# Which weight sums of a feed-forward are made by accumulating transfers, and where the second product stands

## The chip, the cores and the metric

The kernel runs on one core of one Trainium2 chip. The metric is the device time of one execution in microseconds (us), as the median of several executions. One more execution was recorded by the hardware profiler; its rows are quoted below. The engines are named as in the profile: PE (TensorE, the matrix products), DVE (VectorE), ACT (ScalarE), POOL (GpSimd, which here mostly issues transfers that add to their destination) and SP (SyncE, which issues the plain loads).

## The reference, cut to what matters

The block is a mixer part (a short convolution and a retention, merged by gates) and a feed-forward, over 512 tokens of width 1024. The change lies in the feed-forward:

```python
D_MODEL = 1024; SEQ = 512; D_FF = 2816
h2 = rmsnorm(x, g_ffn[l])
x = x + (jax.nn.silu(h2 @ w_ff_gate[l]) * (h2 @ w_ff_up[l])) @ w_ff_down[l]
return rmsnorm(x, g_final)
```

Everything is float32.

## The kernel before

**Products.** Each float32 operand is split into a high and a low part, and one product is three matrix products (high by high, high by low, low by high). On top of that, blocks of four quarter products are done in seven instead of eight, by Strassen's scheme in Winograd's form. With the quarters b11, b12, b21, b22 of the weights, the seven right-hand sides are b11, b21, b22 as they are, and four sums: t1 = b11 + b12, t2 = t1 + b22, t3 = b12 + b22, t4 = t2 + b21 (signs are put on the other side). The names of the products go by these seven.

**Stages.** The inner width 2816 is 11 blocks of 256. Ten of them are done as five "gate and up" quads, two blocks at a time (`("g", 0)` to `("g", 4)`), the eleventh (LONE, `("f", 10)`) as one small quad. The product with the down weights comes in three parts: `("d", 0)`, `("d", 4)`, `("d", 8)`. The order on PE is: quads 0 and 1 interleaved, quad 2, down part 0, quad 3, quad 4, down part 1, the lone quad, down part 2. A quad or one of the first two down parts takes 14 units of weights: seven forms, each in two halves (u = 0 and u = 2) of 128 x 1024 elements. A unit serves 12 matrix products of 128 x 512.

**From load to product.** `plan()` (L64) writes the order of the units by hand. `loads()` (L158) derives from it which quarters SP loads into tiles `raw` (ten buffers), and when. `prefetch_form` (L296) makes a unit: where the form is a sum that isn't made elsewhere, VectorE adds the second quarter into the first one's tile (L307); then ACT writes the high part (`whi`, L208) and VectorE the low part (`wlo`, L209) into one of five pairs of buffers. `take` (L339) keeps two units prefetched beyond the one in use; what stands first in the program has priority, and an engine's instructions run in one fixed order, set when the kernel is built.

**Sums by transfer.** For quad 0 and another matrix all four sums are made in DRAM long ahead (`SUMMED`, L146). For quads 1 to 4, `joined` (L149) says that t3 and t4 come from accumulating transfers: once VectorE has used the tile b12 for t1, POOL issues a transfer that adds b22 to it (that gives t3), and once t2 is split, one that adds b21 to its tile (that gives t4). `late` and `join_late` (L317, the transfer L321) put them one unit later. t1 and t2 are VectorE's. In the down parts and the lone quad all four sums are VectorE's.

**Order in a quad.** In quads 2 to 4 (`quad`, L1301) the products run b11, t1, t2, b21, t3, t4, b22: `first_a` is b11, `rest` the others, with `first_b` (b21) in its middle. The products b11, t2, t3, t4 add up in the same two PSUM banks `a`, so that their state after t2 is copied out by ACT (`snap`, L452) before t3 may go on. The two down parts have the order b11, b21, t1, t2, t3, t4, b22, in `strassen` with `early=True`. Evictions are VectorE's (L1268, L1289, L1298, L465, L477, L488); `gated` (L1224) applies the gate and transposes blocks (L1228, L1229, L1233); `scatter` (L1236) sends the transposed tiles, by 16 small transfers on SP, to where `act_forms_of` (L1172) makes the left-hand sides of the down product from them. `lone` (L1211) does the latter for quad 4 in one go, behind its first eviction.

Of the kernel before, what the change touches and what calls it, by code (L numbers as in the profile page):

```python
# [39 lines left out]
NQ = NFB // 2  # L40
# [14 lines left out]
WIDTH = {"w": 512, "x": 256, "a": 512, "o": 512, "f": 256, "g": 512, "d": 512}  # L55
FORMS = ("b11", "t1", "t2", "b21", "t3", "t4", "b22")

DOWN_FORMS = ("b11", "b21", "t1", "t2", "t3", "t4", "b22")

NEEDS = {"b11": "b11", "b21": "b21", "t1": "b12", "t2": "b22"}  # L60

# [2 lines left out]
def plan():  # L64

    out = []

    def a(name, col):
        out.append(("c", name, 0, 8, col, 256))

    def b(name, row, nk, col, nc):
        out.append(("c", name, row, nk, col, nc))

    def quad(c0, c1):
        for name in FORMS:  # L80
            for u in (0, 2):
                out.append(("q", ("w", c0, c1), name, u, 2))

    for h in range(EARLY):
        for r in (0, 512):
            b("w_in", r, 4, (C_Q + h * QK, C_K + h * QK), 512)
    for h in range(HEADS):
        quad(C_V + h * VD, C_G + h * VD)
        if h >= EARLY:
            a("w_in", C_Q + h * QK)  # L90
            a("w_in", C_K + h * QK)
    for c in (0, 512):
        quad(C_GA + c, C_GR + c)
    for c0, c1 in ((C_XC, C_GC), (C_XC + 256, C_GC + 256), (C_GB, C_GB + 256)):
        for name in FORMS:
            out.append(("q", ("x", c0, c1), name, 0, 4))
    for s in (2, 3):
        for c in (C_XC, C_GC, C_GB):
            a("w_in", c + s * 256)
    for h in range(HEADS):  # L100
        for c in (0, 512):
            b("w_r_out", h * VD, 4, c, 512)
    for kind, name in [("a", x) for x in FORMS[:6]] + [("o", "b11"), ("a", "b22")] + [
            ("o", x) for x in ("t1", "t2", "b21", "b22", "t3", "t4")]:
        for u in (0, 2):
            out.append(("q", (kind,), name, u, 2))
    def f(q, *names):
        for n in names:
            if q == LONE:
                out.append(("q", ("f", q), n, 0, 4))  # L110
            else:
                for u in (0, 2):
                    out.append(("q", ("g", q), n, u, 2))

    def d(q0, n):
        names = FORMS if q0 + n == NQ else DOWN_FORMS
        units = [(name, u) for name in names for u in range(0, n, 2)]
        if q0 + n == NQ:

            i = units.index(("b21", 2))  # L120
            units[i:i + 3] = units[i + 1:i + 3] + units[i:i + 1]
        for name, u in units:
            out.append(("q", ("d", q0), name, u, min(2, n - u)))

    f(0, "b11", "b21")
    f(1, "b11")
    f(0, "t2", "t1", "t3", "t4", "b22")
    f(1, "t1", "t2", "b21", "t3", "t4", "b22")
    f(2, *FORMS)
    d(*FF_PARTS[0])  # L130
    f(3, *FORMS)
    f(4, *FORMS)
    d(*FF_PARTS[1])
    f(LONE, *FORMS)
    d(*FF_PARTS[2])
    return out

# [8 lines left out]
SUMMED = (("g", 0), ("o",))  # L146


def joined(quad, name):  # L149

    return quad[0] == "g" and quad not in SUMMED and name in ("t3", "t4")


def parts(quad):
# [21 lines left out]
def block_kernel(ctx: ExitStack, tc: tile.TileContext, xw0, xw, xT, xtok, wpack, wquad, cols, decs, rot, g_ffn, g_final, out):  # L176
# [15 lines left out]
    def bigtile(dt=F32, n=4):  # L192
        return big.tile([P, n, 512], dt, tag="big", name="big", padded_shape=[P, 4, 512])
# [4 lines left out]
    def bank():  # L198
        return psum.tile([P, 512], F32, tag="bank", name="bank")
# [27 lines left out]
    pos = [0]  # L227
# [5 lines left out]
    def unit():  # L233
        hi = wpool.tile([P, QH], F32R, tag="whi", name="whi")
        lo = wpool.tile([P, QH], F32R, tag="wlo", name="wlo")
        return hi, lo
# [18 lines left out]
    raws = {}  # L255
# [4 lines left out]
    def quarter(quad, name, u):  # L260
        return wquad[next(i for i, x in enumerate(QUARTERS) if x[1:4] == (quad, name, u))]
# [34 lines left out]
    def prefetch_form(quad, f, u, nk):  # L296


        n = nk * WIDTH[quad[0]]
        if quad in SUMMED:  # L300
            here, more = f, None
        else:
            here = {"t1": "b11", "t2": "b11", "t4": "b11", "t3": "b12"}.get(f, f)
            more = {"t1": "b12", "t2": "b22", "t4": "b21", "t3": "b22"}.get(f)
        t = raws[quad, here, u][:, 0:n]
        if more and not joined(quad, f):
            nc.vector.tensor_tensor(out=t, in0=t, in1=raws[quad, more, u][:, 0:n], op=ALU.add)  # L307
        hi, lo = unit()
        split(t, hi[:, 0:n], lo[:, 0:n])
        for g, after, src, add in (("t3", "t1", "b12", "b22"), ("t4", "t2", "b11", "b21")):  # L310
            if f == after and joined(quad, g):
                late.append((pos[0] + 1, raws[quad, src, u], quarter(quad, add, u), n))
        return [(hi, lo)]

    late = []
# [175 lines left out]
    def of(pair, o=0):  # L491
        return lambda k, sl: tuple(t[:, k, sl.start + o:sl.stop + o] for t in pair)
# [169 lines left out]
    for h in range(EARLY):  # L662
# [27 lines left out]
        t = bigtile()  # L690
# [281 lines left out]
    for h in range(HEADS):  # L972
# [5 lines left out]
        t = sg  # L978
# [108 lines left out]
    def behind(i):  # L1087
        if i == 5:
            turn(0, 0)
            return  # L1090
        turn(1, 1)
        po["a"] = [bank(), bank()]
        prod_tm(4, of(M["a11"]), po["a"], True, False, lambda tt: join(tt, 0, po["a"][tt]))
        turn(0, 1)
        form(M, "s1", m32["a22"], m32["a21"], m32["a22"], ALU.subtract)
        form(M, "s2", m32["a22"], m32["a22"], m32["a11"], ALU.subtract)
    strassen(4, zf, merge(0, 0), merge(0, 2), merge(1, 2), merge(1, 0), behind)
    a, d, b = po["a"], [bank(), bank()], [bank(), bank()]
# [40 lines left out]
    names = {"w": ("s2", "s4"), "v": ("s3", "s1"), "a": ("a11", "a12")}  # L1139
# [57 lines left out]
    def lone_gated(th, g, u):  # L1197

        s = t512()
        nc.scalar.activation(s, g, AF.Silu)  # L1200
        if not lone_x:
            lone_x.extend(t512().rearrange("p (b q e t) -> p b q e t", b=2, q=1, e=2) for _ in range(2))
        for b, o in enumerate(lone_x):
            for e in range(2):
                x, y = (t.rearrange("p (e j b r) -> p e b j r", e=2, j=2, b=4)[:, e, 2 * b:2 * b + 2] for t in (u, s))
                z = o[:, :, 0, e, 64 * th:64 * th + 64].rearrange("p b (j r) -> p b j r", j=2)
                nc.vector.tensor_tensor(out=z, in0=x, in1=y, op=ALU.mult)
# [3 lines left out]
    def lone(behind):  # L1211
        got = {}

        def ev11(t):
            got.update(g=t)
            behind()()
        forms = {"a11": XF[0, 0], "a12": XF[1, 0], "a22": XF[1, 1], **{n: XF[n] for n in ("s1", "s2", "s3", "s4")}}
        fm_quad(forms, ev11, lambda ps: lone_gated(1, ps, got["u"]),
                lambda t: got.update(u=t), lambda t: lone_gated(0, got["g"], t))
        act_forms_of(LONE, 1, *lone_x)()  # L1220

    turned = {}
# [41 lines left out]
    def first_b(i):  # L1264
        b = [bank(), bank()]
        prod_tm(4, of(XF[1, 0]), b, True, True)
        for tt, p1 in enumerate(heads_of[i][1]):
            nc.vector.tensor_tensor(out=p1, in0=b[tt], in1=p1, op=ALU.add)  # L1268

    def rest(i, last_first=False, middle=True, behind=None):  # L1270

        a, p1 = heads_of[i]
        d = [bank(), bank()]
        if not last_first:
            prod_tm(4, of(XF["s1"]), d, True)
        prod_tm(4, of(XF["s2"]), a, False)
        u2 = [snap(x) for x in a]
        if last_first:
            prod_tm(4, of(XF["s1"]), d, True)
        if middle:  # L1280
            first_b(i)
        prod_tm(4, of(XF["s3"]), a, False, part=(0,))
        if behind:
            others = behind()
        prod_tm(4, of(XF["s3"]), a, False, part=(2,))
        u3 = [t512(), t512()]
        copies = [nc.scalar.copy(t, x) for t, x in zip(u3, a)]
        for tt in range(2):
            nc.vector.tensor_tensor(out=u3[tt], in0=d[tt], in1=u3[tt], op=ALU.subtract)  # L1289
        if behind:  # L1290
            with tc.issue_after(copies[-1].ins):
                others()
        prod_tm(4, of(XF[1, 1]), a, False, True)
        for tt in range(2):
            gated(i, 2 + tt, a[tt], u3[tt])
        prod_tm(4, of(XF["s4"]), d, False, True)
        for tt in range(2):
            nc.vector.tensor_tensor(out=u2[tt], in0=d[tt], in1=u2[tt], op=ALU.subtract)  # L1298
            gated(i, tt, p1[tt], u2[tt])

    def quad(i, behind, after=None):  # L1301
        first_a(i)
        if after:
            after()
        rest(i, behind=behind)

    first = dram.tile([S, D], F32, name="first_part")
    def add_y(t, nb, half):
# [44 lines left out]
    n = FF_PARTS[-1][1]  # L1353
# [53 lines left out]
    a, d, b = ([bank(), bank()] for _ in range(3))  # L1407
# [122 lines left out]
```

## Time and profile before

| | |
|---|---|
| time, median of 3 runs | 1015.91 us (1015.24 to 1016.36) |
| the profiled execution | 1016.66 us, of which the span from the first to the last instruction is 1014.4 us |
| granted PE clock, mean | 0.996 |
| feed-forward in the trace | from about 686.9 us: quads 0 and 1 to 762.6, quad 2 to 801.9, down part 0 to 840.5, quad 3 to 878.7, quad 4 to 917.2, down part 1 to 955.4, lone quad to 976.3, down part 2 to about 1005 |

The profile's page gives busy times of each engine; a matrix product's end is modelled, so its row shows 0.39 us although the next one starts some 0.23 us later, and real gaps on PE are best read from the starts. A timeline row gives the start, the duration and, in brackets, how long the engine stood idle and what ended the wait. A table of windows gives the busy time of each engine in each stretch.

### The profile page before, as it was taken

What the parts mean: (1) busy time and instruction counts of PE and PEld (TensorE: products, weight loads), DVE (VectorE), ACT (ScalarE), POOL (GpSimd) and SP (SyncE); (2) the same over time, 40 slices, a digit from 0 to 9 for tenths busy, and PEclk for the clock granted to TensorE, in tenths of its full rate; (3) what the DMA queues carried; (4) which work ended last, traced back from release to release, by engine and by line L of the source; (5) the groups of instructions that cost most, each with busy time, mean ns of one, the idle gap of its engine ahead of it and who ended that gap; (6) DMA issues with size and microseconds to landing.
All of it is one profiled execution on the core that took longest, in us unless ns stands there. A gap on an engine that the chain in (4) does not pass through costs nothing.

```text
span 1014.4 us, 13342 instructions
## 1 busy us (share of the span) xinstructions
PE 1002.5 (99%) x4746; PEld 838.4 (83%) x4746; DVE 894.2 (88%) x1163; ACT 547.4 (54%) x736; POOL 154.3 (15%) x246
## 2 busy tenths in 40 slices
PE   9999999999999999999999999999999999999996
PEld 7888888888888998888888888888887888888884
DVE  7878898979798888697989997999988996989897
ACT  7547655553655455343452325577665555574664
POOL 0030221222122004112221200011101000003202
PEclk9999999999999999999999999999999999999998
DMA  9525587695767658839687865467677369486953
GB/s 352 189 76 184 185 289 219 206 306 177 231 191 257 222 217 276 332 131 331 154 306 257 288 233 180 127 202 231 167 228 152 139 208 267 107 248 127 274 140 104
DMA packets 60642, 215.87 MB, mean 213 GB/s; under 512 B 8928, under 2 KB 9056, under 8 KB 55968
## 3 DMA queue, kind: packets, MB, share of 16 engines
q1 hardware_dynamic: 42592, 144.73, 41.7%
q0 software_dynamic: 17696, 70.01, 25.6%
q8 instruction: 37, 0.61, 0.3%
q10 hardware_dynamic: 288, 0.29, 0.1%
q14 instruction: 29, 0.24, 0.1%
HBM read 171.21 MB, written 57.41 MB: 225 GB/s over the span
## 4 chain that ended last, share of the span: by engine, by line
PE 87%; DVE 8%; issue 2%; SPq 2%; DMA 1%; ACT 1%; POOL 0%; POOLq 0%; DVEq 0%; ACTq 0%
PE bank L445 48%; PE bank L360 10%; PE bank L361 10%; PE bank L362 10%; PE bank L401 8%; DVE wlo L209 2%; SPq L1243 2%; DVE raw L307 1%; DMA big<-turned 1%; DVE turned L1233 1%; DVE t L1229 1%; DVE t L1182 0%; DVE big L209 0%; PE bank L501 0%; ACT whi L208 0%
## 5 line engine op out<-in xcount | busy, mean ns | idle before, releaser
L208 ACT CAST whi<-raw 128x1024 fp32r<-128x1024 f32 (+2 forms) x299 | 301.8, 1028 | 239.0 <-PE bank L445 73.5
L209 DVE TENSOR_TENSOR wlo<-raw,whi 128x1024 fp32r<-128x1024 f32 (+2 forms) x300 | 350.8, 1189 | 69.6 <-ACT whi L208 68.9
L445 PE MATMUL bank<-whi,xform 128*128 128x512 f32 x1056 | 330.5, 390 | 0.0
L445 PEld LDWEIGHTS bank<-whi,xform 128*128 128x128 f32 x1056 | 198.0, 188 | 42.2 <-DVE xform L209 1.0
L445 PE MATMUL bank<-wlo,xform 128*128 128x512 f32 x528 | 205.8, 390 | 0.5 <-DVE wlo L209 0.5
L445 PE MATMUL bank<-whi,big 128*128 128x512 f32 x596 | 187.5, 390 | 0.3 <-ACT t L452 0.3
L307 DVE TENSOR_TENSOR raw<-raw 128x1024 f32<-128x1024 f32 x112 | 132.2, 1198 | 0.8
L445 PEld LDWEIGHTS bank<-whi,big 128*128 128x128 f32 x596 | 111.7, 188 | 24.5 <-ACT t L452 1.1
L445 PEld LDWEIGHTS bank<-wlo,xform 128*128 128x128 f32 x528 | 99.1, 188 | 22.1 <-DVE wlo L209 1.7
L445 PE MATMUL bank<-wlo,big 128*128 128x512 f32 x298 | 116.1, 390 | 0.1
L452 ACT COPY t<-bank 128x512 f32<-128x512 f32 x95 | 55.5, 587 | 70.8 <-PE bank L445 55.8
L360 PE MATMUL bank<-big,whi 128*128 128x512 f32 x220 | 85.7, 390 | 0.0
L362 PE MATMUL bank<-big,wlo 128*128 128x512 f32 x220 | 85.6, 389 | 0.0
L361 PE MATMUL bank<-big,whi 128*128 128x512 f32 x220 | 85.6, 389 | 0.0
L445 PEld LDWEIGHTS bank<-wlo,big 128*128 128x128 f32 x298 | 55.9, 188 | 12.0 <-DVE wlo L209 0.6
L401 PE MATMUL bank<-xform,whi 128*128 128x256 f32 x304 | 55.3, 283 | 0.2 <-ACT t L452 0.2
L360 PE MATMUL bank<-whi,big 128*128 128x512 f32 x128 | 49.8, 389 | 0.0
L361 PE MATMUL bank<-wlo,big 128*128 128x512 f32 x128 | 49.8, 389 | 0.0
L362 PE MATMUL bank<-whi,big 128*128 128x512 f32 x128 | 49.8, 389 | 0.0
L362 PEld LDWEIGHTS bank<-big,wlo 128*128 128x128 f32 x220 | 41.3, 188 | 8.7
L361 PEld LDWEIGHTS bank<-big,whi 128*128 128x128 f32 x220 | 41.3, 188 | 8.5
L360 PEld LDWEIGHTS bank<-big,whi 128*128 128x128 f32 x220 | 41.3, 188 | 8.5
(211 smaller groups left out, 1395.1 us busy)
## 6 DMA issues: line engine op xcount, KB each, us to landing
raw<-wquad SPq DMA_DIRECT2D x140, 512.0 KB, 5.2
raw<-wpack SPq DMA_DIRECT2D x42, 512.0 KB, 5.9
raw<-wquad POOLq DMA_DIRECT2D x16, 512.0 KB, 6.4
t_g<-wquad POOLq DMA_DIRECT2D x12, 512.0 KB, 7.7
z<-t POOLq DMA_DIRECT2D x24, 256.0 KB, 5.6
t_o<-wquad POOLq DMA_DIRECT2D x12, 512.0 KB, 6.7
zform<-z POOLq DMA_DIRECT2D x6, 1024.0 KB, 7.1
big<-turned SPq DMA_DIRECT2D x80, 64.0 KB, 4.5
```

The costliest lines, as they stand in the source:

```text
L208: first = (round or nc.scalar.copy)(hi, src)
L209: low_of[0] = nc.vector.tensor_tensor(out=lo, in0=src, in1=hi.bitcast(F32), op=ALU.subtract)
L307: nc.vector.tensor_tensor(out=t, in0=t, in1=raws[quad, more, u][:, 0:n], op=ALU.add)
L360: nc.tensor.matmul(ps, lh, rh, start=first, stop=False)
L361: nc.tensor.matmul(ps, lh, rl, start=False, stop=False)
L362: nc.tensor.matmul(ps, ll, rh, start=False, stop=last)
L401: nc.tensor.matmul(o, l[:, c], r[:, k], start=start and s == 0 and k == 0 and i == 0, stop=stop and k == 3 and i == 2, skip_group_check=True)
L445: nc.tensor.matmul(pss[tt], l, r[:, c], start=start and k == 0 and i == 0, stop=stop and k == n - 1 and i == 2, skip_group_check=True)
L452: nc.scalar.copy(t, ps)
L1229: nc.vector.tensor_tensor(out=s, in0=u, in1=s, op=ALU.mult)
L1233: nc.vector.transpose(t[:, :, :, j, :].rearrange("p q i r -> p i q r"), s.rearrange("p (i q c) -> p i q c", i=4, q=4)[:, :, 2 * h:2 * h + ...
L1243: nc.sync.dma_start(o[32 * q:32 * q + 32], turned[i][q // 2][32 * b:32 * b + 32, q % 2].rearrange("c i j r -> c (i j r)"))
```

## The change

In `joined`, the quads 1 to 4 stay and the first down part comes in. Of the four sums of these five blocks, t1 is now made by a transfer that adds b12 to the tile of b11 once b11 is split, t4 by one that adds b21 as before, and t2 and t3 by VectorE. In quads 2 to 4 the product with b21 comes second, as in the down parts, and their loads follow that order. In `lone`, the second half of quad 4's left-hand sides is placed behind a later eviction.

```diff
-DOWN_FORMS = ("b11", "b21", "t1", "t2", "t3", "t4", "b22")
+EARLY_FORMS = ("b11", "b21", "t1", "t2", "t3", "t4", "b22")
...
-    f(2, *FORMS)
+    f(2, *EARLY_FORMS)
     d(*FF_PARTS[0])
-    f(3, *FORMS)
-    f(4, *FORMS)
+    f(3, *EARLY_FORMS)
+    f(4, *EARLY_FORMS)
     d(*FF_PARTS[1])
...
-def joined(quad, name):
-    return quad[0] == "g" and quad not in SUMMED and name in ("t3", "t4")
+def joined(quad):
+    return quad not in SUMMED and (quad[0] == "g" or quad == ("d", 0))
...
-        if more and not joined(quad, f):
+        if more and not (joined(quad) and f in ("t1", "t4")):
             nc.vector.tensor_tensor(out=t, in0=t, in1=raws[quad, more, u][:, 0:n], op=ALU.add)
         hi, lo = unit()
         split(t, hi[:, 0:n], lo[:, 0:n])
-        for g, after, src, add in (("t3", "t1", "b12", "b22"), ("t4", "t2", "b11", "b21")):
-            if f == after and joined(quad, g):
-                late.append((pos[0] + 1, raws[quad, src, u], quarter(quad, add, u), n))
+        add = {"b11": "b12", "t2": "b21"}.get(f)
+        if add and joined(quad):
+            late.append((pos[0] + 1, raws[quad, "b11", u], quarter(quad, add, u), n))
...
         def ev11(t):
-            got.update(g=t)
-            behind()()
+            got.update(g=t, others=behind())
...
         fm_quad(forms, ev11, lambda ps: lone_gated(1, ps, got["u"]),
-                lambda t: got.update(u=t), lambda t: lone_gated(0, got["g"], t))
+                lambda t: (got.update(u=t), got["others"]()), lambda t: lone_gated(0, got["g"], t))
...
     def quad(i, behind, after=None):
         first_a(i)
         if after:
             after()
-        rest(i, behind=behind)
+        first_b(i)
+        rest(i, middle=False, behind=behind)
```

More of the change, by code (lines that the diff above doesn't have):

```diff
@@ L115, in d @@
     def d(q0, n):
-        names = FORMS if q0 + n == NQ else DOWN_FORMS
+        names = FORMS if q0 + n == NQ else EARLY_FORMS
         units = [(name, u) for name in names for u in range(0, n, 2)]
```

## The prediction

> **What bounds the kernel now.** I began with the busy times on the page and then asked for windows of five stages of the feed-forward: quad 2, down part 0, quad 3, quad 4, down part 1.
>
> ```profile
> PE 1002.5 (99%) x4746; PEld 838.4 (83%) x4746; DVE 894.2 (88%) x1163; ACT 547.4 (54%) x736; POOL 154.3 (15%) x246
> ...
> core 0: us, PE busy (x) PEld busy (x) DVE busy (x) ACT busy (x) POOL busy (x), PEclk, DMA share, GB/s
> 762.60:801.90 39.30, 38.76 (x170) 31.46 (x169) 35.91 (x47) 25.06 (x32) 3.51 (x4) 1.00 0.72 188
> 801.90:840.50 38.60, 38.29 (x169) 31.35 (x169) 37.41 (x40) 18.69 (x22) 1.76 (x2) 1.00 0.52 159
> 840.50:878.70 38.20, 38.20 (x170) 31.65 (x169) 29.61 (x37) 21.74 (x29) 1.75 (x2) 1.00 0.68 197
> 878.70:917.20 38.50, 38.50 (x170) 31.56 (x170) 35.05 (x46) 24.59 (x32) 3.50 (x4) 1.00 0.73 192
> 917.20:955.40 38.20, 38.20 (x170) 31.37 (x169) 36.42 (x40) 18.49 (x22) 12.33 (x15) 1.00 0.89 215
> ```
>
> PE is the bound: full clock, hardly a gap. What the change can win is what is missing to an uninterrupted PE, so I looked at the starts of matrix products in PE's timeline. Between two starts of the regular pattern (three products) lie 0.68 us; a unit of 12 takes 2.72 us, the 168 of a stage 38.1 us. The five stages last 192.8 us together and need 190.4: **2.4 us is the whole ceiling** there. The gaps:
>
> ```profile
> 767.72 0.61 PE L445 MATMUL bank<-whi,xform 128*128 128x512 f32 x2
> 768.42 0.50 PE L445 MATMUL bank<-wlo,xform 128*128 128x512 f32 x1
> 768.75 0.63 PE L445 MATMUL bank<-whi,xform 128*128 128x512 f32 x2
> ...
> 770.82 0.61 PE L445 MATMUL bank<-whi,xform 128*128 128x512 f32 x2
> 771.89 0.50 PE L445 MATMUL bank<-wlo,xform 128*128 128x512 f32 x1 [0.46 <-DVE wlo L209]
> ...
> 773.39 0.39 PE L445 MATMUL bank<-wlo,xform 128*128 128x512 f32 x1
> 773.62 0.61 PE L445 MATMUL bank<-whi,xform 128*128 128x512 f32 x2
> 774.07 0.39 PE L445 MATMUL bank<-wlo,xform 128*128 128x512 f32 x1
> ...
> 824.62 0.39 PE L445 MATMUL bank<-whi,big 128*128 128x512 f32 x1
> 825.32 0.50 PE L445 MATMUL bank<-whi,big 128*128 128x512 f32 x1 [0.31 <-ACT t L452]
> ...
> 886.44 0.61 PE L445 MATMUL bank<-whi,xform 128*128 128x512 f32 x2
> 887.00 0.50 PE L445 MATMUL bank<-wlo,xform 128*128 128x512 f32 x1
> ...
> 939.76 0.83 PE L445 MATMUL bank<-whi,big 128*128 128x512 f32 x2
> 940.43 0.40 PE L445 MATMUL bank<-wlo,big 128*128 128x512 f32 x1
> ```
>
> (773.39 to 774.07 is the 0.68.) Start to start minus 0.227 us for each product gives 0.25 us at 768.2 and 0.62 at 771.3 (the two units of t1 in quad 2), 0.47 at 824.9 (down part 0, from t2 to t3), 0.11 at 886.9 (second unit of t1 in quad 4), 0.22 in the pair at 939.76 (down part 1, t2 to t3). After the first four one product comes 0.10 us late as well (768.42 to 768.75 is 0.33). So: quad 2 about 1.1, down part 0 0.6, quad 4 0.2, down part 1 0.2.
>
> Next, why. For quad 2 the VectorE timeline:
>
> ```profile
> 762.31 1.21 DVE L307 TENSOR_TENSOR raw<-raw 128x1024 f32<-128x1024 f32 x1
> 763.44 1.28 DVE L1298 TENSOR_TENSOR t<-bank,t 128x512 f32<-128x512 f32 x2
> 764.64 1.28 DVE L1229 TENSOR_TENSOR t<-t,t 128x512 f32<-128x512 f32 x2
> 765.84 1.41 DVE L1233 STREAM_TRANSPOSE turned<-t 128x256 f32<-128x256 f32 x4
> 767.18 1.18 DVE L209 TENSOR_TENSOR wlo<-raw,whi 128x1024 fp32r<-128x1024 f32 x1
> 768.29 2.35 DVE L307 TENSOR_TENSOR raw<-raw 128x1024 f32<-128x1024 f32 x2
> 770.61 2.36 DVE L209 TENSOR_TENSOR wlo<-raw,whi 128x1024 fp32r<-128x1024 f32 x2
> ```
>
> Quad 1's evictions and transposes (763.44 to 767.18) meet quad 2's sums: the low part of t1's first unit ends at 768.36, that of the second at about 771.8, and PE stands for both. A sum costs 1.14 us, start to start. At 825 the reason differs, as ACT's timeline shows:
>
> ```profile
> 823.73 1.05 ACT L208 CAST whi<-raw 128x1024 fp32r<-128x1024 f32 x1 [0.82 <-DVE raw L307]
> 824.68 0.58 ACT L452 COPY t<-bank 128x512 f32<-128x512 f32 x1
> ...
> 896.29 1.05 ACT L208 CAST whi<-raw 128x1024 fp32r<-128x1024 f32 x1 [0.40 <-DMA raw<-wquad]
> ```
>
> t2 and t3 add up in one bank, so ACT has to copy t2's state out before t3 goes on. A cast that waited for VectorE's sum stood in ACT's queue ahead of the second copy, and PE went on as it ended at 825.26.
>
> **The change, part by part.**
>
> (1) *t1 leaves VectorE in quads 2 and 4, and b21 stands between.* The units after b11 are then two of b21, with no sum, and two of t1, with none. In quad 2, with evictions done at 767.2, two low parts of b21 and two of t1 are through by 767.2 + 4 x 1.14 = 771.8, where PE wants t1 at 762.6 + 4 x 2.72 = 773.5 and its second unit at 776.2. Both gaps go: -1.1 us in quad 2 and, by the same sequence, -0.2 in quad 4. Quad 3 has no gap to give.
>
> (2) *The sum comes back for t3.* Per quad VectorE keeps four sums; nothing is saved in its total. They stand behind t1 now, with two units more before them, and what they delay next is t3's cast and the copies of (5). In quad 1, whose order stays, the sums of t1 move to t3, where VectorE now waits:
>
> ```profile
> 742.57 1.22 DVE L209 TENSOR_TENSOR wlo<-raw,whi 128x1024 fp32r<-128x1024 f32 x1 [1.99 <-ACT whi L208]
> 745.17 1.22 DVE L209 TENSOR_TENSOR big<-big 128x1024 fp32r<-128x1024 f32 x1 [1.37 <-ACT big L208]
> ```
>
> 3.4 us of idle time take 2.3 us of sums: nothing. Without that cover it would cost at most those 2.3 us.
>
> (3) *Down part 0 loses four of its eight sums on VectorE*, 4.6 us of 37.4 busy in 38.6. t4's cast no longer waits for VectorE; the 0.6 us at 825 has lost its cause, but t4's cast now waits for a transfer. I take -0.35, between 0 and -0.6.
>
> (4) *The transfers.* Four more, and all shorter in lead. The rows of L321:
>
> ```profile
> L321 POOL DMA_DIRECT2D raw<-wquad x16: 870/873/947, 721.1 to 892.0; - x16
> DMA to landing us min/median/max: 5.3/6.4/11.2
> 888.43 0.88 POOL L321 DMA_DIRECT2D raw<-wquad  x1 [2.77 <-DVE wlo L209]
> ```
>
> On POOL 4 x 0.87 = 3.5 us join 1.76 busy in down part 0, and no other POOL work of that stage is queued behind. 2.1 MB join 159 GB/s x 38.6 us = 6.1 MB: 213 GB/s, what down part 1 carries (215) without a stall by landing. Each sum now has four units, 10.9 us, from its tile's split to its own product (t4 had six). Issue comes about 0.4 us after the low part, landing at 6.4, cast and low part take 2.2: 9.0 of 10.9 us, had VectorE no lead at all; with the worst landing 13.8, so 2.9 us of lead are then needed. For t1 of quad 2 the row
>
> ```profile
> 756.32 1.22 DVE L209 TENSOR_TENSOR wlo<-raw,whi 128x1024 fp32r<-128x1024 f32 x1
> ```
>
> puts the first split's end at 757.5, 16 us ahead of its product at 773.5.
>
> The Trainium skill has another duration for such a transfer: "DMA: Bandwidth & Descriptors", section "Anatomy of one DMA — SWDGE (gpsimd) path", gives 2.0 us and bytes / 436e3, an estimate of 3.2 us for 524288 bytes; by that, rival A would fall away and the sum would be nearer to rival B. The sixteen landings here, 5.3 to 11.2 us, speak against it. In the other direction, "SBUF — State Buffer", section "SBUF: two separate sides", says that GpSimd can be locked out by a VectorE instruction while it writes descriptors; read strictly, each issue could grow by one VectorE instruction and rival A would be about even. The issues' 870 to 947 ns beside a VectorE that is busy nine tenths of the time don't show it, and its chance stays as below.
>
> (5) *New: t2 goes straight into t3 in quads 2, 3 and 4*, as b21's two units no longer lie between. ACT's two copies of the banks come under the path in three more places. With ACT free they fit: a copy takes 0.59 us and each bank has half a unit, 1.36 us. A cast in front adds up to 1.05. Bounds for a place: 0 (copies fit) and the 0.6 us of down part 0; I take 0.25, near down part 1's 0.2, since sums are less dense in a quad. Three places: **+0.75**.
>
> (6) *Lone quad.* Six VectorE instructions of 0.6 us for quad 4's left-hand sides go behind a later eviction. Cover: the product of s4 and of the next stage's b11 lies between them and their use. I take 0; uncovered they cost up to 3.6 us, and the stage has only this to give back:
>
> ```profile
> 955.40:976.30 20.90, 20.69 (x171) 20.26 (x170) 19.55 (x27) 12.60 (x18) 1.73 (x2) 1.00 0.88 235
> ```
>
> that is 0.2 us.
>
> Sum: -1.1 - 0.2 - 0.35 + 0.75 + 0 = **-0.9 us**. The profiled execution took 1016.66 us (span 1014.4), so its like would take 1015.8; the median of the runs lies 0.75 us lower at 1015.91, and the forecast for it is **1015.0 us**.
>
> **The rivals.** *A, slower: casts of t4 that wait for a transfer hold ACT's copies.* ACT's order is fixed. If t4's cast stands before the copies of t2's state, PE waits at t3 for a landing. The row at 896.29 is such a cast that waited; today nothing hangs on it. Its transfer was issued at 888.43, 1.3 us before its t2 product (about 889.7); cast and copy after it would have ended at 896.29 + 1.05 + 0.59 = 897.9, where t3 would have come two units after 889.7, at 895.1: 2.8 us of stall. It decides where the transfer is issued less than 1.3 + 2.8 = 4.1 us before the t2 product. In quad 2 I get t2's low part at 771.8 + 2 x 1.14 = 774.1, issue at 774.5 and product at 762.6 + 6 x 2.72 = 778.9: 4.4 us, and 3.2 if the two evictions of b21's product (1.2 us) come first. That is near the edge. At two places (quads 2 and 4, which follow a quad): -0.9 + 5.6 = +4.7, **1020.6 us**. For it: the same cast stood between the two copies in down part 0. Against it: down part 0 and quad 3 start with VectorE ahead, and if only the second copy waits, 1.4 us a place (half a unit less) are left. Chance 0.17.
>
> *B, faster: the copies fit everywhere.* -1.1 - 0.2 - 0.6, and 0.2 more in down part 1 if the casts ahead of it come earlier: -2.1, **1013.8 us**. For it: VectorE has less to do early in each block. Against it: both places where t2 meets t3 today have a gap. Chance 0.11.
>
> *C, the change does nothing on balance:* the gaps of t1 come back as gaps of t3, three places at 0.5 (near down part 0's 0.6) against 1.65 won: **1015.8 us**. Chance 0.22.
>
> **How the numbers follow.** Forecast 0.50, C 0.22, A 0.17, B 0.11. A measurement of this kernel can tell about 0.2%, 2.0 us, from no change. Forecast and C lie within it almost wholly; B ends right at that edge (0.08 beyond it, as the ceiling is 2.4 us), A mostly (0.15), and 0.02 are left for (6) uncovered. That gives faster 0.08, same 0.75, slower 0.17. The range goes from the ceiling, 1015.9 - 2.4 = 1013.5, to 1019.0, A with 1.4 us at each of three places and 0.5 at the fourth, less the 1.65 won; A with more is left out.
>
> **What would show it.** Step 1: no gap on PE at t1 of quads 2 and 4, the low part of t1 ended ahead of its product. Step 3: some 4.6 us less VectorE in down part 0, no gap beyond 0.3 us at its t3. Step 5: gaps of 0 to 0.6 us where t3 begins, with ACT's copy (L452) as releaser. Rival A: ACT casts waiting for the transfer at L321, and PE behind L452 for over 1 us. Step 6: no gap at the start of down part 2. The forecast is wrong if PE waits at t1 for a transfer, or if loads on SP come later in the new order.

## The result and the profile after

| | before | after |
|---|---|---|
| time, median (6 runs each, side by side) | 1016.39 us (1015.24 to 1016.80) | 1030.01 us (1026.37 to 1031.83) |
| ratio, 95% interval | | 1.0130 (1.0111 to 1.0149) |
| profiled execution | 1016.66 us, span 1014.4 | 1030.07 us, span 1028.3 |

The change makes the kernel 1.3% slower. In the code after the change, L1217 to L1304 of the listing above are one lower; L307, L321, L445 and L452 are the same.

The first view is again the table of windows by stage (quad 2, down part 0, quad 3, quad 4, down part 1), with the columns of the table in the prediction: the stretch, its length, then busy time and count of PE, weight loads, VectorE, ACT and POOL, then granted clock, DMA share and GB/s.

```profile
761.70:809.10 47.40, 39.81 (x170) 32.51 (x170) 37.18 (x48) 23.07 (x30) 3.81 (x5) 0.93 0.60 156
809.10:852.20 43.10, 39.97 (x169) 32.62 (x168) 29.94 (x33) 18.68 (x22) 3.50 (x5) 0.96 0.71 184
852.20:890.40 38.20, 38.20 (x170) 31.61 (x170) 31.95 (x38) 23.51 (x30) 3.50 (x4) 1.00 0.74 207
890.40:930.50 40.10, 38.30 (x169) 31.38 (x168) 34.87 (x48) 23.09 (x30) 1.75 (x2) 1.00 0.62 170
930.50:968.60 38.10, 38.10 (x170) 31.54 (x169) 35.51 (x39) 18.29 (x22) 12.31 (x15) 1.00 0.91 215
```

The five stages now last 206.9 us instead of 192.8: +14.1, where the span grew by 13.9. Quad 2 gives 8.1 of it, down part 0 4.5, quad 4 1.6; quad 3 and down part 1 run without a gap. Two things are to be seen besides the lengths: the clock is below 1.00 in the two longest stages, and PE's busy time is only 2.4 us more than before in sum. The rest is waiting. Whom PE waits for stands in its list of waits (total us, times, longest):

```profile
PE bank L445 <- ACT t L452: 12.5, 3, 7.6
```

Three waits, all for ACT's copy of a bank, all at the start of t3's product. In PE's timeline the largest looks like this:

```profile
783.29 0.39 PE L445 MATMUL bank<-whi,xform 128*128 128x512 f32 x1
791.27 0.79 PE L445 MATMUL bank<-whi,xform 128*128 128x512 f32 x1 [7.59 <-ACT t L452]
...
793.57 0.93 PE L445 MATMUL bank<-whi,xform 128*128 128x512 f32 x2
794.34 0.39 PE L445 MATMUL bank<-wlo,xform 128*128 128x512 f32 x1
```

From start to start, less 0.23 for a product, PE stands still for 7.75 us. The seven products behind it take 3.07 us instead of 1.59, as the clock is halved: 1.5 us more. The same reading gives 3.29 us at 834.15 (down part 0) with 1.7 of slow products behind it, and 1.95 at 914.04 (quad 4) with none. Stops 13.0, slow clock 3.2, less the 2.1 of old gaps (1.1, 0.6, 0.2, 0.2) that are gone: 14.1. The account closes.

What held the copy is in ACT's timeline, in the same quad, in down part 0 and in quad 4:

```profile
783.63 1.04 ACT L208 CAST whi<-raw 128x1024 fp32r<-128x1024 f32 x1 [2.15 <-DMA raw<-wquad]
784.58 1.56 ACT L208 CAST big<-big 128x1024 fp32r<-128x1024 f32 x2
789.69 1.04 ACT L208 CAST whi<-raw 128x1024 fp32r<-128x1024 f32 x1 [3.55 <-DMA raw<-wquad]
790.64 1.07 ACT L452 COPY t<-bank 128x512 f32<-128x512 f32 x2
...
828.21 1.05 ACT L208 CAST whi<-raw 128x1024 fp32r<-128x1024 f32 x1 [4.22 <-DMA raw<-wquad]
832.57 1.04 ACT L208 CAST whi<-raw 128x1024 fp32r<-128x1024 f32 x1 [3.31 <-DMA raw<-wquad]
833.52 1.07 ACT L452 COPY t<-bank 128x512 f32<-128x512 f32 x2
...
908.30 1.05 ACT L208 CAST whi<-raw 128x1024 fp32r<-128x1024 f32 x1 [3.07 <-DMA raw<-wquad]
909.26 1.05 ACT L208 CAST big<-big 128x1024 fp32r<-128x1024 f32 x1
911.94 0.62 ACT L208 CAST big<-big 128x512 fp32r<-128x512 f32 x1 [1.64 <-DMA big<-turned]
912.47 1.04 ACT L208 CAST whi<-raw 128x1024 fp32r<-128x1024 f32 x1
913.41 1.06 ACT L452 COPY t<-bank 128x512 f32<-128x512 f32 x2
```

Each time both casts of t4, and in the quads two casts for the down product's left-hand sides as well, stand ahead of the copies of t2's state. The casts of t4 wait for a landing, and the copies, which need nothing but PE, wait behind them. In quad 4 the last of these waits is put down to the scatter's transfers (`big<-turned`), which the casts of the left-hand sides need; the second transfer for t4 had landed by then (7.2 us after its issue at 904.34, at 911.5). By an estimate from these rows (911.5, then a cast of 0.95 and a copy of 0.59) it alone would have held PE until some 913.1, about 1.0 us; the scatter made 1.95 of it. With t4 by VectorE and with shorter transfers for t4 (both below) these casts wait for no scatter in quad 4, so the load of t4's transfers is likely to delay that too. The transfers themselves, on POOL:

```profile
777.29 0.88 POOL L321 DMA_DIRECT2D raw<-wquad  x1 [15.29 <-DVE wlo L209]
778.40 0.89 POOL L321 DMA_DIRECT2D raw<-wquad  x1 [0.24 <-issue]
...
822.42 0.87 POOL L321 DMA_DIRECT2D raw<-wquad  x1 [13.31 <-DVE wlo L209]
823.56 0.87 POOL L321 DMA_DIRECT2D raw<-wquad  x1 [0.26 <-DMA first_part<-t]
...
861.03 0.88 POOL L321 DMA_DIRECT2D raw<-wquad  x1 [13.21 <-DVE wlo L209]
...
902.61 0.87 POOL L321 DMA_DIRECT2D raw<-wquad  x1 [13.05 <-DVE wlo L209]
```

In quad 2 the second transfer is issued at 778.40 and its cast can begin at 789.69: 11.3 us. That cast (1.05) and one copy (0.59) end at 791.3, which is where PE goes on. A product of t2 begins 24 x 0.227 = 5.44 us before t3 is due; so the lead, from the first issue to t2's product, can be set beside the stop:

| place | t2's product | first issue | lead, us | stop at t3, us |
|---|---|---|---|---|
| quad 2 | 778.1 | 777.29 | 0.8 | 7.75 |
| down part 0 | 825.4 | 822.42 | 3.0 | 3.29 |
| quad 4 | 906.6 | 902.61 | 4.0 | 1.95 |
| quad 3 | 868.6 | 861.03 | 7.5 | 0 |

(Quad 3: 852.24, the start of its first product, and six units of 2.72.) Three of the kernels below keep full transfers for t4 and this order of ACT in some block, and the same reading of them gives leads of 0.3, 1.6, 2.2, 2.9 and 3.9 us with stops of 8.00, 6.29, 4.82, 3.55 and 2.49: in all these places a shorter lead goes with a longer stop. Why the lead is so short in quad 2 stands in VectorE's timeline:

```profile
771.09 3.49 DVE L307 TENSOR_TENSOR raw<-raw 128x1024 f32<-128x1024 f32 x3
774.49 1.28 DVE L1267 TENSOR_TENSOR t<-bank,t 128x512 f32<-128x512 f32 x2
775.69 3.49 DVE L209 TENSOR_TENSOR wlo<-raw,whi 128x1024 fp32r<-128x1024 f32 x3
```

The two sums of t2, the first sum of t3 and two evictions come first; only then the low parts, the first of which, done at 776.8, lets POOL issue.

### The profile page after: what moved, and what is told of

Its sections match the earlier page's. It is cut to its first block, busy times and chain, and to the rows that moved or that the text cites. A ratio compares the mean times of both kernels' runs of the same rounds, so it can differ in the third digit from the quotient of the medians.

```text
span 1028.3 us, 13353 instructions
## 1 busy us (share of the span) xinstructions
PE 1004.3 (98%) x4746; PEld 840.4 (82%) x4746; DVE 891.0 (87%) x1159; ACT 546.7 (53%) x736; POOL 155.5 (15%) x250
## 4 chain that ended last, share of the span: by engine, by line
PE 86%; DVE 5%; DMA 3%; issue 3%; SPq 1%; ACT 1%; POOL 0%; POOLq 0%; ACTq 0%; DVEq 0%
PE bank L445 47%; PE bank L360 10%; PE bank L361 10%; PE bank L362 10%; PE bank L401 8%; DMA raw<-wquad 2%; SPq L1242 1%; DVE wlo L209 1%; DMA big<-turned 1%; DVE raw L307 0%; DVE turned L1232 0%; DVE big L209 0%; DVE t L1228 0%; PE bank L501 0%; ACT whi L208 0%
## 5 line engine op out<-in xcount | busy, mean ns | idle before, releaser
L209 DVE TENSOR_TENSOR wlo<-raw,whi 128x1024 fp32r<-128x1024 f32 (+2 forms) x300 | 352.7, 1193 | 88.9 <-ACT whi L208 88.2
L445 PE MATMUL bank<-whi,xform 128*128 128x512 f32 x1056 | 331.8, 391 | 9.4 <-ACT t L452 9.4
L445 PEld LDWEIGHTS bank<-whi,xform 128*128 128x128 f32 x1056 | 198.7, 188 | 52.4 <-ACT t L452 10.2
L445 PE MATMUL bank<-wlo,xform 128*128 128x512 f32 x528 | 205.9, 390 | 0.0
L445 PE MATMUL bank<-whi,big 128*128 128x512 f32 x596 | 188.8, 392 | 3.4 <-ACT t L452 3.1
L445 PEld LDWEIGHTS bank<-whi,big 128*128 128x128 f32 x596 | 112.7, 189 | 28.1 <-ACT t L452 3.6
L307 DVE TENSOR_TENSOR raw<-raw 128x1024 f32<-128x1024 f32 x108 | 127.6, 1203 | 2.8 <-DMA raw<-wquad 2.1
L445 PE MATMUL bank<-wlo,big 128*128 128x512 f32 x298 | 116.8, 392 | 0.0
L445 PEld LDWEIGHTS bank<-wlo,xform 128*128 128x128 f32 x528 | 99.5, 189 | 20.5
L452 ACT COPY t<-bank 128x512 f32<-128x512 f32 x95 | 55.0, 586 | 61.4 <-PE bank L445 43.3
L445 PEld LDWEIGHTS bank<-wlo,big 128*128 128x128 f32 x298 | 56.3, 189 | 11.9 <-DVE wlo L209 0.3
```

The costliest lines, as they stand in the source:

```text
L209: low_of[0] = nc.vector.tensor_tensor(out=lo, in0=src, in1=hi.bitcast(F32), op=ALU.subtract)
L445: nc.tensor.matmul(pss[tt], l, r[:, c], start=start and k == 0 and i == 0, stop=stop and k == n - 1 and i == 2, skip_group_check=True)
L452: nc.scalar.copy(t, ps)
```

## The experiments

All but one, the kernel before with the edit of the lone quad alone, start from the changed kernel. The theories that the expectations weigh are these. **K**: two things together; the transfer for t4 comes too late, as only four units lie between t2's split and t4's product and VectorE makes t2's low part late, and ACT's fixed order turns that lateness into a stop already at the copies of t2's state. **Q**: the order of ACT's queue alone; with the copies ahead, nothing is lost. **L**: the landing alone; t4 is late in any order of ACT. **M**: the two transfers in a row into one tile (t1's, then t4's). **B**: the bytes and the number of the transfers. **D**: VectorE is late, whatever the transfers do. **O**: the early b21 itself.

### Copies ahead of the casts of t4

```diff
-        split(t, hi[:, 0:n], lo[:, 0:n])
+        with (tc.issue_after(last_copy[0].ins) if f == "t4" and quad in HELD else ExitStack()): split(t, hi[:, 0:n], lo[:, 0:n])
...
-        nc.scalar.copy(t, ps)
+        last_copy[0] = nc.scalar.copy(t, ps)
```

`HELD` are quads 2 to 4 and down part 0; `last_copy` is ACT's latest copy of t2's state.

> The changed kernel with one thing forced: in quads 2 to 4 and down part 0 the casts of t4 (and with them the first casts of the down product's left-hand sides) stand behind the two copies of t2's state in ACT's order. Transfers and sums are as in the changed kernel. Theory Q (ACT's queue: a cast waiting for a transfer holds the copies, and PE waits for the copies): the gaps of 7.8, 3.3 and 2.0 us where t3 begins go to at most 0.6 us each, and with them the slow stretches behind the first two; time 1014 to 1018 us, with new gaps of up to 1 us where t4 begins. Rival L (the transfers land too late whatever stands behind them): the gaps only move to the start of t4, with low parts of t4 as releasers, and most of the time stays, 1021 to 1029 us. Rival D (VectorE is late, the copies only show it): no change, 1027 to 1031 us.

1027.83 us; ratio to before 1.0123 (1.0105 to 1.0140). PE's list of waits now reads:

```profile
PE bank L445 <- ACT t L1286: 6.5, 3, 3.2
PE bank L445 <- ACT whi L208: 1.8, 2, 1.0
PE bank L445 <- ACT t L452: 1.7, 1, 1.7
```

The wait at L452 has nearly gone, and another has come at L1286, the copies of t3's state one boundary later. ACT's timeline shows why:

```profile
788.81 2.94 ACT L208 CAST whi<-raw 128x1024 fp32r<-128x1024 f32 x3 [1.21 <-DMA raw<-wquad]
791.65 1.06 ACT L1286 COPY t<-bank 128x512 f32<-128x512 f32 x2
```

The casts, one of them waiting, still stand ahead of a pair of copies, only of the next. So moving these casts alone (Q, as this edit tries it) doesn't give the time back; the stop in quad 2 shrank from 7.75 to 2.44 us, but others came. The time lies in L's range, but none of the stops has a low part of t4 as its releaser, by which L was to be known.

### The same, with b22's casts behind t3's copies

```diff
-        with (tc.issue_after(last_copy[0].ins) if f == "t4" and quad in HELD else ExitStack()): split(t, hi[:, 0:n], lo[:, 0:n])
+        with (tc.issue_after(last_copy[0].ins) if f in ("t4", "b22") and quad in HELD else ExitStack()): split(t, hi[:, 0:n], lo[:, 0:n])
...
-        copies = [nc.scalar.copy(t, x) for t, x in zip(u3, a)]
+        copies = [nc.scalar.copy(t, x) for t, x in zip(u3, a)]; last_copy[0] = copies[-1]
```

> The kernel with the copies of t2's state ahead, and in addition the casts of b22 behind the copies of t3's state in quads 2 to 4 and down part 0. Theory Q (the queue alone): the gaps of 2.4, 1.1 and 3.4 us at t4 shrink to below 0.8 us each, and the time falls to 1016 to 1022 us. Theory K: casts that wait for t1's and t4's landings still hold ACT for some 2 to 7 us a block, so what is put off shows at the next product that ACT serves; 1023 to 1029 us.

1023.12 us; 1.0079 (1.0062 to 1.0095), 0.79% of the 1.30%. Quad 2's stop is gone: its two transfers for t4 are issued where they were (777.20 and 778.31) and the second takes 9.4 us to land, but PE loses only 0.2 us there, at t3 and t4 together. So in quad 2 late landings cost next to nothing once the copies stand ahead of the casts that wait; L falls there. The time left is lost elsewhere. The two largest stops are 2.04 us at 808.82 and 1.73 at 888.19; the rows for the first:

```profile
802.36 1.85 POOL L321 DMA_DIRECT2D raw<-wquad  x2 [23.15 <-DVE wlo L209]
807.72 1.04 ACT L208 CAST whi<-raw 128x1024 fp32r<-128x1024 f32 x1 [7.87 <-DMA raw<-wquad]
808.82 0.74 PE L445 MATMUL bank<-whi,big 128*128 128x512 f32 x2 [1.88 <-ACT whi L208]
```

Down part 0 begins at 800.79, so this is the start of its second product, and the transfers are those for its t1: they were issued 1.6 us behind the block's start, where after the change the first one was issued 5.2 us ahead of it (803.92, start 809.10). The casts behind b22's on ACT come later with them, which would do this; it wasn't tried by itself. A third stop, 1.33 us at 910.96 in quad 4, is again of the old kind, a cast of t4 that waits for its landing (1.98 us) ahead of the copies of t3's state. So the edit gives Q's gain in quad 2 and takes part of it back by being late for the next block; it doesn't say what a repaired order without that cost would take.

### t4 by VectorE, t1 by transfer

```diff
-        if more and not (joined(quad) and f in ("t1", "t4")):
+        if more and not (joined(quad) and f == "t1"):
...
-        add = {"b11": "b12", "t2": "b21"}.get(f)
+        add = {"b11": "b12"}.get(f)
```

> The changed kernel, but t4 is added by VectorE in quads 1 to 4 and down part 0; only t1 comes from a transfer. ACT's order keeps the casts of t4 ahead of the copies of t2's state. Theory Q: the casts no longer wait for a landing but for a sum of 1.14 us, so the gaps at t3 shrink to 0 to 2 us each; 1015 to 1021 us. Rival L: gone as well, 1015 to 1018 us. Rival D: VectorE gets 8 sums (9.1 us) more in the quads and 2 (2.3 us) more in down part 0, so gaps grow; 1030 us and above.

**1012.99 us; 0.9973 (0.9962 to 0.9985)**: faster than both. Its windows by stage (quad 2 to down part 1) are 38.1 us each, which is what the 168 products need:

```profile
760.90:799.00 38.10, 38.10 (x169) 31.46 (x168) 37.93 (x49) 23.40 (x30) 1.75 (x2) 1.00 0.60 166
799.00:837.10 38.10, 38.10 (x169) 31.50 (x168) 33.14 (x37) 18.90 (x22) 1.77 (x2) 1.00 0.61 169
837.10:875.20 38.10, 38.10 (x170) 31.54 (x169) 33.73 (x40) 23.28 (x30) 1.69 (x2) 1.00 0.61 186
875.20:913.30 38.10, 38.10 (x170) 31.55 (x169) 37.23 (x49) 23.29 (x30) 0.08 (x1) 1.00 0.51 156
913.30:951.40 38.10, 38.10 (x170) 31.55 (x169) 35.50 (x39) 18.28 (x22) 12.34 (x15) 1.00 0.91 217
```

VectorE is busy 37.93 of 38.10 us in quad 2, and PE loses nothing. ACT's timeline at the boundary from t2 to t3:

```profile
779.97 1.57 ACT L208 CAST big<-big 128x1024 fp32r<-128x1024 f32 x2
781.43 1.04 ACT L208 CAST whi<-raw 128x1024 fp32r<-128x1024 f32 x1
782.38 0.57 ACT L452 COPY t<-bank 128x512 f32<-128x512 f32 x1
783.32 0.59 ACT L452 COPY t<-bank 128x512 f32<-128x512 f32 x1 [0.36 <-PE bank L445]
```

The same casts stand ahead of the copies as after the change; none waits for a landing, and the second copy has time to wait for PE. The new order and t1 by transfer are harmless; t4 by transfer is the cause. D, by which more sums on VectorE should cost more, falls, and so does O. Together with the kernel before this one it shows the two parts of K in quad 2: without the wait for a landing, or without the copies behind the casts that wait, the stop is gone.

### The new order with the sums of before

`joined` takes a name again and gives t3 and t4 of the quads to transfers, as in the listing of before; the order stays new, and down part 0 is VectorE's.

> Only the order: b21 second in quads 2 to 4 (and the lone quad's edit), sums as in the kernel before (t1, t2 by VectorE, t3 and t4 by transfers, down part 0 all by VectorE). Theory Q: the order alone puts casts of t4, which wait for a transfer issued only two to four units earlier, ahead of the copies; gaps of 2 to 8 us at t3 of quads 2 and 4 remain, none over 0.7 us in down part 0; 1020 to 1030 us. Rival M (the chain of two transfers in a row, t1 then t4, makes the lateness): with t1 by VectorE the landing is in time, gaps below 1 us; 1014 to 1018 us.

1028.13 us; 1.0120 (1.0105 to 1.0135): stops of 4.82 us at 788.86 and of 3.55 at 909.70, both at L452, none in down part 0. Here t4's tile gets a single transfer, so M falls: the chain isn't needed for the loss. The leads are 2.2 us in quad 2 and 2.9 in quad 4. In quad 2 the last wait ahead of the copies was for the scatter, 1.94 us, as in quad 4 above.

### The old order with the sums of the change

`EARLY_FORMS` back to `FORMS` for quads 2 to 4 in `plan`, and `rest(i, behind=behind)` in `quad`; down part 0 keeps the change.

> The changed kernel's sums (t1 and t4 by transfers, t2 and t3 by VectorE, down part 0 too), but quads 2 to 4 in the old order with b21 after t2. Theory K (a sum by transfer costs time where fewer units lie between the split of its tile and its own product than landing, cast and low part take; ACT's queue only decides at which product PE stands): t4 has six units again and no wait, t1 has two instead of four, 5.4 us against some 9, so PE stands at t1 of quads 2 and 4, 2 to 5 us each, and down part 0 keeps its 3 us; 1020 to 1030 us. Rival O (the early b21 itself is at fault): 1014 to 1019 us, with the gap of down part 0 alone.

1029.05 us; 1.0138 (1.0121 to 1.0154). The time is what K forecast, its places are so only in part. In quad 4, t1 now stops PE for 1.45 us at 896.98, where its cast had waited 8.13 us for a landing, and for 1.03 at 898.24, for its low part. In quad 2 nothing waits at t1; the 1.08 us at 773.77 are at the start of t2, for a low part that VectorE makes behind three sums, and 0.81 at 885.34 and 2.00 at 890.19 are waits for low parts too. No stop is left at t3 in the quads, but one in down part 0 takes 8.00 us (830.64, at L452), where after the change it took 3.29. Its lead there is 0.3 us (first issue 816.89, t2's product 817.2): t1's transfers were issued later (797.44 and 801.76, start 800.87), VectorE stood 1.89 us for a cast of t1, and the sums behind it came later. The loss has moved to where t4 by transfer still has four units.

### Down part 0 back to VectorE

```diff
-    return quad not in SUMMED and (quad[0] == "g" or quad == ("d", 0))
+    return quad not in SUMMED and (quad[0] == "g")
```

> The changed kernel without down part 0 among the sums by transfer (its four sums are VectorE's, as before). Theory Q: the gap of 3.3 us at its t3 and the 1.7 us of slow products behind it go, 0.6 us as in the kernel before comes back; the gaps of quads 2 and 4 stay; about 4.4 us less than the changed kernel, 1024 to 1027 us. Rival: the gap in down part 0 is only an echo of quad 2's delay or of its dense transfers and stays at 2 to 4 us; 1028 to 1031 us.

1023.95 us; 1.0084 (1.0061 to 1.0107), by the two ratios some 4.7 us less than the change. The stop of down part 0 is gone; 6.29 us at 790.55 and 2.49 at 909.64 are left in the quads, with leads of 1.6 and 3.9. As in quad 4 after the change, the last wait ahead of the copies in quad 4 is for the scatter (2.13 us).

### Shorter transfers for t4

```diff
-            late.append((pos[0] + 1, raws[quad, "b11", u], quarter(quad, add, u), n))
+            late.append((pos[0] + 1, raws[quad, "b11", u], quarter(quad, add, u), n if add == "b12" else 256))
```

> The changed kernel with ACT's order untouched, but the transfers for t4 add only 256 of the 1024 columns, so that t4 is left without three quarters of its sum. Theory K: they land 2 to 4 us sooner, and the gaps at t3 shrink by about as much, from 7.8, 3.3 and 2.0 us to 2 to 5, 0 to 1 and 0 to 0.5 us, the slow products behind the first with them; 1016 to 1022 us. Rival D (VectorE's lateness or the order of the queue whatever the landing): no change, 1027 to 1031 us.

The transfers add 256 of the 1024 columns, so this kernel leaves out three quarters of t4's sum. 1018.37 us; 1.0031 (1.0018 to 1.0044). The issues in quad 2 stand where they stood, at 777.32 and 778.43; ACT's timeline behind them:

```profile
782.36 1.57 ACT L208 CAST big<-big 128x1024 fp32r<-128x1024 f32 x2
784.55 1.05 ACT L208 CAST whi<-raw 128x1024 fp32r<-128x1024 f32 x1 [0.62 <-DMA raw<-wquad]
785.50 1.07 ACT L452 COPY t<-bank 128x512 f32<-128x512 f32 x2
```

The order of ACT is unchanged; the second landing comes 6.1 us after its issue instead of 11.3, and the stop is 2.39 us instead of 7.75; in down part 0 it is 0.84 instead of 3.29, and in quad 4 there is none. With the issues and the order held, shorter transfers take away some 70% of the stop in quad 2: what sets its length is the landing.

### t1 and t3 by transfer

```diff
-        if more and not (joined(quad) and f in ("t1", "t4")):
+        if more and not (joined(quad) and f in ("t1", "t3")):
...
-        add = {"b11": "b12", "t2": "b21"}.get(f)
+        add = {"b11": "b12", "t1": "b22"}.get(f)
```

(and `b12`'s tile as the target of the second)

> The changed kernel with the same number of transfers, but those of t4 given to t3: t1 and t3 by transfers, t2 and t4 by VectorE, in quads 1 to 4 and down part 0. The tile of t3 is b12, which nothing writes before, so its transfer can go as soon as b12 is loaded, some eight units ahead of its product. Theory K: no gaps, like the kernel with t4 by VectorE, 1012 to 1014 us. Rival B (the number of transfers and their bytes): at least half of the changed kernel's loss stays, 1020 us and above.

1017.24 us; 1.0017 (1.0007 to 1.0026). As many transfers as after the change, and one stop of 2.08 us (784.86, quad 2) is left: B, by which their number should cost as much wherever they go, falls. K's own number was missed too, by this stop. ACT waits there for no landing but for VectorE's sum of t4, and VectorE had waited earlier, for 0.77 and 1.70 us, for casts of t1, whose first transfer was issued at 760.17 instead of 756.05. POOL had been free since 754.7, so it wasn't the queue behind t3's transfers: the issue waited for a low part of b11 that VectorE made later. Why VectorE came later in this kernel isn't shown.

### All sums of these blocks by VectorE, in the new order

```diff
-    return quad not in SUMMED and (quad[0] == "g" or quad == ("d", 0))
+    return False
```

> The changed kernel with no transfer among the sums of quads 1 to 4 and down part 0: all four sums are VectorE's, b21 second. Theory K (only lateness of transfers costs): no waits for landings, but VectorE gets eight sums (9.1 us) a quad where the changed kernel has four; with some 35 us of work in 38.1 us of products it is then the bound in quads 2 and 4 by 1 to 3 us each, quads 1 and 3 can take some from their neighbours; 1015 to 1022 us. If VectorE's order alone were the trouble: more than the changed kernel, 1030 us and above.

1019.53 us; 1.0037 (1.0024 to 1.0051). PE waits 3.5 us in four places for low parts (`wlo` L209), none longer than 1.1. VectorE is the bound then, mildly. The transfers for t1 are worth 0.64% against this (1.0037 to 0.9973), some 6.5 us; those for t4 cost 1.6% on top (0.9973 to 1.0130), some 16 us.

### The edit of the lone quad, taken away and alone

Two kernels: t4 by VectorE as above with `lone` as before the change, and the kernel before with the edit of `lone` alone.

> The kernel with t4 by VectorE, without the edit of the lone quad (quad 4's left-hand sides made in one go behind the first eviction, as in the kernel before). The edit costs and brings little (prediction, step 6): 1012.5 to 1014 us. If it is what makes that kernel faster than the one before by more than the gaps of quads 2 and 4 and down part 0: 1014 to 1015.5 us, with PE gaps of 0.4 us or more in the lone quad or at the start of down part 2.

> The kernel before with only the lone quad's edit. By step 6 of the prediction no change: 1015 to 1016 us. If the edit fills PE's gaps there: 0.4 to 1.5 us less, 1014.4 to 1015.4 us. If it makes down part 2 late: above 1016.5 us.

1013.32 us, 0.9976 (0.9967 to 0.9986), where it was 0.9973 with the edit; and 1015.32 us, 1.0000 (0.9991 to 1.0009). The edit changes nothing that can be measured.

## Why the prediction was wrong

**Step 1 was right.** No gap is left at t1 in quads 2 and 4. With the old order t1 of quad 4 waits for its transfer again (1.45 us and 1.03 for the low part), so b21 in between has a part in it there; in quad 2 t1 has no gap in the old order either, and the transfer alone suffices.

**Step 2 failed, and this is where the error begins.** It said that VectorE's sums of t3 delay "t3's cast and the copies of (5)". They delayed t2's low part, on which t4's transfer hangs. The prediction had that low part end at 774.1 in quad 2, as if VectorE took sum and low part of each unit in turn. VectorE took three sums and the evictions first: the second sum of t2 and the first of t3 (2.3 us) and two evictions (1.2) came ahead of it, the row of sums began 0.7 us earlier than reckoned, and it ended at 774.1 + 2.3 + 1.2 - 0.7 = 776.9. So the issue came at 777.29 instead of 774.5, and t2's product at 778.1 instead of 778.9, as the quad itself began 0.9 us earlier: 4.4 us of lead became 0.8. t1's transfer, harmless at t1, had a share in that. Its second unit was issued at 761.12, its cast began only at 768.86, after 5.86 us of waiting, and VectorE stood 2.30 us for that cast. With t4 by VectorE it was issued at 758.99 and nothing waited for it; there the row of sums begins 7.6 us behind the quad's start (768.54), after the change 9.4 us (771.09). A sum that costs no time in VectorE's total can cost it in its order.

**Step 4 mis-sized the landing.** It took 6.4 us and 0.4 from low part to issue; in quad 2 the second of two transfers issued 1.1 us apart took 11.3, in down part 0 9.0 (823.56 to 832.57). The "worst landing" with its need of 2.9 us of lead was written down, but as a bound, and it was met where the DMA engines were full: their busy share was 0.97 while PE stood in quad 2 and 1.02 in down part 0 (the rows are below). The shorter transfers show that this term sets the length of the stop in quad 2.

By the estimate of 3.2 us that the prediction drew from the Trainium skill ("DMA: Bandwidth & Descriptors", "Anatomy of one DMA — SWDGE (gpsimd) path") the second unit would have landed at 781.6 instead of some 789.7, and little of ACT's wait would be left. The measurement decides against it: L321's twenty transfers take 5.3 to 11.2 us after the change too, with a median of 5.7. The lock-out that the prediction drew from the Trainium skill ("SBUF — State Buffer", "SBUF: two separate sides") didn't show either; the issues took 870 to 947 ns as before.

**Rival A was the case.** Its mechanism, its two places in the quads and its threshold hold: it gave 4.1 us of lead as the point from which it decides, and leads of 4.0, 3.0 and 0.8 stopped PE for 1.95, 3.29 and 7.75 us, while 7.5 didn't. That a lead of 4.0, so near to 4.1, stopped PE for as long is in part luck: about half of that stop is the scatter's. What was wrong was its size and its chance. The lead in quad 2 came out at 0.8 instead of the estimated 3.2 to 4.4 (step 2). It priced one cast ahead of the copies; both units' casts and two casts of left-hand sides were there, so that the second landing and the scatter count. Down part 0 was held to be safe, since VectorE starts ahead there; its lead was 3.0. And the halved clock (3.2 us) was in no term. 1020.6 became 1030. With a lead estimated right at the threshold, and both errors of the estimate going one way (later), 0.17 was too little.

**Step 5 failed with it.** It gave 0.25 us, at most 0.6, for each new boundary from t2 to t3; the three took 7.75, 0 and 1.95. What the bound left out is a cast ahead of the copies that waits for a landing. The copies as such it priced too high: with t4 by VectorE none of these boundaries has a gap, as copies fit as long as no cast ahead of them waits, and **rival B** (1013.8) is in effect what that kernel shows with 1013.0.

**Step 3** removed the sums: down part 0 has 29.94 us of VectorE instead of 37.41, of which four sums are 4.6; three further instructions fell into its neighbours. It saved nothing, as t4's cast, freed from VectorE, waited for its transfer instead. **Step 6** was right.

**What stays open:** why the second of two transfers lands 4.4 us (down part 0) and 6.1 us (quad 2) after the first although it is issued 1.1 us later. Full DMA engines and the order in the queue would both do it, and no run here separates them.

## What to carry to other kernels

Before a sum or a load goes to a transfer, count from the end of the instruction that allows its issue, in that engine's real order, to its use, with the longest landing that the trace has; then ask what stands behind the instruction that will wait. On an engine with a fixed order a late operand costs at the first thing queued behind it, here a copy of a bank, a whole product earlier than its own use. And of several sums give away the one whose transfer can go well ahead of its own product, and measure each further one: with t1 given away the kernel was 0.3% faster than before, with t3 as well 0.2% slower than before, with t4 as well 1.3% slower.

## What was not expected of the hardware

PE's clock falls after stops of a few microseconds, and in steps of 3.4 us. The windows of the changed kernel around two stops (columns as above; granted clock is the third number from the end):

```profile
783.60:787.40 3.80, 0.08 (x1) 0.00 (x0) 2.69 (x3) 2.51 (x3) 0.00 (x0) 1.00 0.97 280
787.40:794.20 6.80, 2.93 (x7) 2.35 (x8) 3.71 (x5) 2.96 (x4) 0.00 (x0) 0.50 0.48 185
794.20:797.60 3.40, 3.40 (x16) 2.79 (x16) 2.04 (x3) 1.59 (x2) 0.00 (x0) 1.00 0.56 199
831.00:834.10 3.10, 0.02 (x1) 0.00 (x0) 0.46 (x1) 1.53 (x3) 0.00 (x0) 1.00 1.02 370
...
835.20:838.60 3.40, 3.40 (x10) 2.66 (x9) 2.36 (x2) 0.33 (x1) 0.00 (x0) 0.50 0.69 228
```

In down part 0 the clock is full when PE resumes at 834.15, falls 1.0 us later and stays at half for 3.4 us: the window holds ten products, cut ones at its edges included, where one at full clock holds sixteen. The Trainium skill describes such a gate: "TensorE: Matmul & The Clock Gate", section "Part 1: The HAM clock gate (the "warmup" mystery)", has a free-running window of 3413 ns, and half clock after an idle one. The lengths agree (3.4 and 6.8 us). But an idle window wasn't needed. The stop of 2.08 us in the kernel with t1 and t3 by transfer had its half clock, that of 2.49 us in quad 4 of the kernel without down part 0's transfers had none. First the one, then the other, in windows of 3.4 us up to the moment that decides:

```profile
782.40:785.80 3.40, 1.48 (x7) 0.93 (x6) 3.40 (x4) 3.40 (x6) 0.00 (x0) 1.00 0.91 299
785.80:789.20 3.40, 3.40 (x10) 2.63 (x9) 2.59 (x4) 0.44 (x1) 1.76 (x2) 0.50 1.01 377
```

```profile
908.00:911.40 3.40, 1.76 (x8) 1.45 (x9) 2.95 (x4) 3.03 (x5) 0.00 (x0) 1.00 1.01 370
911.40:914.80 3.40, 3.40 (x17) 2.80 (x16) 2.30 (x3) 1.64 (x2) 0.00 (x0) 1.00 0.76 282
```

PE busy for 1.48 of 3.4 us lost the clock, busy for 1.76 kept it: in these runs the limit lies near half of a window, and whether a stop of 2 to 2.5 us is followed by 1.7 us more depends on where it falls in the window. (The edges of the second kernel's windows are counted in steps of 3.413 us: its clock changes at 795.32 and next at 1017.19, 65 such steps later.)
